# The first memory-key projection of a decoder trunk: one panel of 512 columns behind eight zero products

## The chip, the cores and the metric

The kernel runs on one core of one Trainium2 chip. A core has a matrix engine (TensorE, PE in the profile; its weight loads are PEld), a vector engine (VectorE, DVE), a scalar engine (ScalarE, ACT), GpSimd (POOL) and SyncE (SP). Each engine works through its own instructions in order. SP issues almost all transfers; ACT issues a few. The metric is the time of one execution on the device, in microseconds (us); less is better.

## The reference, cut to what matters

The reference is a two-layer decoder trunk on 256 tokens of width 2048. The first layer uses gated linear attention, the second a forgetting attention, and both also attend into 256 memory tokens. The change touches only how the memory keys of the first layer are made:

```python
mem_n = rmsnorm(mem, norm_mem)
for i in range(DEPTH):
    mk, mv = memory_kv(mem_n, mem_w_kv[i])      # (256 x 2048) @ (2048 x 1024): 512 columns of keys, 512 of values
    h = rmsnorm(x, norm_mix[i])
    x = x + mixer(h, mk, mv, ...)
    x = x + conv_ffn(rmsnorm(x, norm_ffn[i]), ...)
return rmsnorm(x, norm_final)
```

## The kernel before, in words

All weights lie in one packed array `wp`, in the order in which they are used, cut into panels and each panel into units of at most 128 x 1024 numbers (512 KB). `_panels` (line 51) lists the panels, `_layout` (line 108) their units. The first panels are: two panels of 256 columns for the keys of layer 0 (`mk`, 0, 0 and 0, 1), one of 512 columns for its values (`mv`, 0), then the same for layer 1, then the projections of the first mixer.

Every product is done in split precision. `load_unit` (line 178) loads a unit into `raw` and ACT rounds it to `whi` (line 189); `split_unit` (line 192) has DVE form the rest `wlo = raw - whi` (line 198). The activations are split the same way by `split` (line 283): ACT writes the high half (line 290), DVE the low half (line 291), side by side in one tile of 2 x 256. In a `proj_fm` panel (line 201) the weights are the stationary operand. For each of 16 chunks of 128 input rows and each block of 128 columns, `product` (line 220) issues two matmuls: `whi` against both halves (512 columns, line 223, or 226 for the last one) and `wlo` against the high half (256 columns, line 224). In this text such two matmuls are a **pair**. In a `proj_tm` panel (line 236) the activations are stationary and each chunk takes three matmuls of 512 columns for each of two blocks of tokens (lines 260 to 262).

Buffers: `raw` has 4, `whi` and `wlo` 3 each; the accumulators `acc` (pool `pacc`) are four banks of PSUM in all. A `proj_fm` panel takes two of them and a `proj_tm` panel two, so one panel's results can be read out while the next one is computed into the other two.

The start of the kernel (lines 404 to 466): `take_mem` (line 407) loads the memory tokens `mt`, in two pieces of two chunks and then three of four, each ahead of the weights that go with it, and splits them into `A`, scaled by the norm's gain from `gains`. The read-out of the first two panels is `mk_out` (line 415): ACT copies one half of the bank to `mk` (line 419), DVE adds the other half (line 420). Only after both is the bank free. `first_out` (line 432) also issues the squares of the memory tokens for its norm: four ACT squares of 128 x 1024 (line 439) and three DVE sums (line 441). Then the tokens `x` come in as 16 transfers of 128 KB (`xf`, line 451), and are split into `B` (line 456, through 290 and 291).

The order of instructions on each engine is fixed when the kernel is built, by a scheduler that is told priorities (`tc.high_priority`) and a few orderings (`tc.issue_after`); line order alone doesn't give it. Semaphores then hold each instruction until its inputs are there and its output buffer is free. A held instruction holds everything behind it on its engine. SP uses eight completion lanes in turn, so at most eight transfers are under way; a load of `raw` is also held until DVE has finished with the buffer's last unit.

Of the kernel before, what the change touches and what calls it, by code (L numbers as in the profile page):

```python
# [12 lines left out]
F32 = mybir.dt.float32  # L13
F32R = mybir.dt.float32r
I32 = mybir.dt.int32
AF = mybir.ActivationFunctionType
ALU = mybir.AluOpType
PSUM = bass.MemoryType.PSUM

P = 128  # L20
T = 256
D = 2048
KC = D // P
# [4 lines left out]
MEM_H = 4  # L28
# [9 lines left out]
AHEAD = 300  # L38

OG_EARLY = 2  # L40


G_Q, G_K, G_V = 0, 1024, 2048
# [7 lines left out]
def _panels():  # L51

    full = list(range(KC))
    out = []

    def fm(key, w, c0, kcs=full, second=None):
        cols = [(c0, 256)] if second is None else [(c0, 128), (second, 128)]  # L60
        out.append((key, w, kcs, cols, 4))

    def tm(key, w, c0, n, kcs=full):
        out.append((key, w, kcs, [(c0, n)], 2))

    for l in range(2):
        for j in range(2):
            fm(("mk", l, j), ("mem_w_kv", l), j * 256)
        tm(("mv", l), ("mem_w_kv", l), 512, 512)
    out.append((("glr",), ("gla_w_in", 0), full, [("twice", G_R, RANK)], 8))  # L70
    for j in range(2):
        fm(("mq", 0, j), ("gla_w_in", 0), G_MQ + j * 256)
    for h in range(GLA_H):
        fm(("gq", h), ("gla_w_in", 0), G_Q + h * DK)
        fm(("gk", h), ("gla_w_in", 0), G_K + h * DK)
        for j in range(OG_EARLY if h == GLA_H - 1 else 0):
            fm(("og", j), ("gla_w_in", 0), G_OG + j * 256)
# [24 lines left out]
    for f in range(4):  # L102
        tm(("wo", 1, f), ("fox_w_out", 0), f * 512, 512, late)
    ffn(1)
    return out
# [30 lines left out]
def _trunk(ctx: ExitStack, tc: tile.TileContext, xt, xtok, memt, wp, wgu, gns, gfin, cnv, par, msk, out):  # L136
    nc = tc.nc
# [6 lines left out]
    pacc = ctx.enter_context(tc.tile_pool(name="pacc", bufs=4, space=PSUM))  # L144
    pwork = ctx.enter_context(tc.tile_pool(name="pwork", bufs=1, space=PSUM))

    S.preload_act_table_set("natural_log_exp_and_others")
    gains = const.tile([P, G_N], F32, name="gains")
    with tc.high_priority(offset=2 * AHEAD):
        nc.sync.dma_start(gains, gns)  # L150
    part = const.tile([P, C_N], F32, name="part")
    mask = const.tile([P, M_N], F32, name="mask")
    ident = mask[:, M_ID : M_ID + P]
# [4 lines left out]
    def gain(name, i):  # L158
        c = C_GAIN[name] + i
        return gains[:, c : c + 1]  # L160
# [6 lines left out]
    bufB = [const.tile([P, 2, T], F32R, name=f"B{i}") for i in range(KC)]  # L167
    mk = [const.tile([P, MEM_H, T], F32, name=f"mk{l}") for l in range(2)]
    mv = [const.tile([P, 2, MEM_H * HD], F32, name=f"mv{l}") for l in range(2)]

    loads, casts = [], []

# [19 lines left out]
    def split_unit(unit, pieces=1, before=None, pool=wpool):  # L192
        with tc.high_priority(offset=AHEAD):
            raw, hi, w = load_unit(unit, pieces, before, pool)
            lo = pool.tile([P, NUNIT], F32R, name="wlo", tag="wlo", bufs=3)
            for i in range(pieces):
                s = slice(i * w // pieces, (i + 1) * w // pieces)
                V.tensor_tensor(lo[:, s], raw[:, s], hi[:, s].bitcast(F32), ALU.subtract)  # L198
        return hi, lo

    def proj_fm(key, src, evac, before=None):

        units = where[key]
        total = sum(len(u[1]) for u in units)
        acc = [pacc.tile([P, 512], F32, name="acc", tag="acc") for _ in range(2)]
        base = min(min(u[1]) for u in units)
        done = 0
        for n, unit in enumerate(units):
            if before is None:
                hi, lo = split_unit(unit)  # L210
            else:
                hi, lo = split_unit(unit, 1 if n else 2, lambda half: before(n, half))
            for j, kc in enumerate(unit[1]):
                for c in range(2):
                    product(acc[c], c, total - 1, done, src[kc - base], hi, lo, j)
                done += 1
        for c in range(2):
            evac(c, acc[c])

    def product(a, c, last, done, both, hi, lo, j):  # L220
        s = slice(j * 256 + c * P, j * 256 + (c + 1) * P)
        if done < last:
            TE.matmul(a, hi[:, s], both, start=done == 0, stop=False)  # L223
        TE.matmul(a[:, :T], lo[:, s], both[:, 0, :], start=False, stop=False)  # L224
        if done == last:
            TE.matmul(a, hi[:, s], both, start=False, stop=True)  # L226
# [177 lines left out]
    with tc.tile_pool(name="load", bufs=1) as lp:  # L404
        mt = [lp.tile([P, 4, T], F32, name=f"mt{i}") for i in range(4)]

        def take_mem(g, half):
            n = 2 if g == 0 else 4
            if n == 2 or half == 0:
                i = half * 2  # L410
                nc.sync.dma_start(mt[g][:, i : i + n, :], memt[g, :, i : i + n, :])
                for i in range(i, i + n):
                    split(bufA, 4 * g + i, mt[g][:, i, :], gain("mem", 4 * g + i))

        def mk_out(l, j):
            def evac(c, a):
                o = mk[l][:, 2 * j + c, :]
                if l == 0:
                    S.activation(o, a[:, T:], AF.Copy)
                    V.tensor_tensor(o, o, a[:, :T], ALU.add)  # L420
                    if c == 1 and j == 1:
                        for f in range(MEM_H):
                            V.tensor_tensor(mk[0][:, f, :], mk[0][:, f, :], nrm.row(), ALU.mult)
                else:
                    V.tensor_tensor(o, whole(a), nrm.row(), ALU.mult)

            return evac

        def mv_out(l):
            return lambda b, a: S.activation(mv[l][:, b, :], a, AF.Copy, scale=nrm.col()[:, b : b + 1])  # L430

        def first_out(c, a):
            mk_out(0, 0)(c, a)
            if c == 1:
                nc.sync.dma_start(mask[:, :M_FOX], msk[:, :M_FOX])
                sq, acc = [lp.tile([P, 4, T], F32, name=n) for n in ("sq4", "ssq4")]
                with tc.issue_after(casts[-1].ins):
                    for g in range(4):
                        S.activation(sq if g else acc, mt[g], AF.Square)
                        if g:  # L440
                            V.tensor_tensor(acc, acc, sq, ALU.add)
                V.tensor_tensor(acc[:, :2, :], acc[:, :2, :], acc[:, 2:, :], ALU.add)
                V.tensor_tensor(acc[:, 0, :], acc[:, 0, :], acc[:, 1, :], ALU.add)
                nrm.acc = acc[:, 0, :]

        proj_fm(("mk", 0, 0), bufA, first_out, before=take_mem)
        proj_fm(("mk", 0, 1), bufA, mk_out(0, 1))
        xf = [lp.tile([P, T], F32, name=f"xf{i}") for i in range(KC)]
        with tc.issue_after(loads[-1].ins):
            for i in range(KC):  # L450
                nc.sync.dma_start(xf[i], xt[i])
            nc.sync.dma_start(part, par)
            nc.sync.dma_start(mask[:, M_FOX:], msk[:, M_FOX:])
        proj_tm(("mv", 0), bufA, mv_out(0))
        for i in range(KC):
            split(bufB, i, xf[i], gain("mix0", i))
        for j in range(2):
            proj_fm(("mk", 1, j), bufA, mk_out(1, j))
            if j == 0:
                with tc.issue_after(loads[-1].ins):  # L460
                    for f in range(4):
                        nc.sync.dma_start(x[f], xtok[f])
                for f in range(4):
                    for b in range(2):
                        nx.add(f, b)
        proj_tm(("mv", 1), bufA, mv_out(1))
# [445 lines left out]
```

## Time and profile before

| | |
|---|---|
| three timed runs | 2315.9, 2314.12, 2314.14 us; median 2314.14 us |
| the profiled execution | 2315.51 us, of which the span from first to last instruction is 2313.7 us |
| DVE busy | 1608.0 us (69%) |
| ACT busy | 1254.2 us (54%) |
| DMA, mean over the span | 187 GB/s |
| mean granted TensorE clock | 0.998 |

All times inside the profile count from the span's start. A row of the timeline gives the start, the duration, the engine, the line in the kernel, the operation, the tile written and the tiles read, and how many like it follow one another; a bracket at its end tells how long the engine was idle before it and what it waited for. Durations of neighbours on one engine overlap by some tens of nanoseconds up to half of a matmul, so the pace of a row of instructions is read from start to start. The granted clock (PEclk) is the share of its full clock that TensorE was allowed.

### The profile page before, as it was taken

What the parts mean: (1) busy time and instruction counts of PE and PEld (TensorE: products, weight loads), DVE (VectorE), ACT (ScalarE), POOL (GpSimd) and SP (SyncE); (2) the same over time, 40 slices, a digit from 0 to 9 for tenths busy, and PEclk for the clock granted to TensorE, in tenths of its full rate; (3) what the DMA queues carried; (4) which work ended last, traced back from release to release, by engine and by line L of the source; (5) the groups of instructions that cost most, each with busy time, mean ns of one, the idle gap of its engine ahead of it and who ended that gap; (6) DMA issues with size and microseconds to landing.
All of it is one profiled execution on the core that took longest, in us unless ns stands there. A gap on an engine that the chain in (4) does not pass through costs nothing.

```text
span 2313.7 us, 32663 instructions
## 1 busy us (share of the span) xinstructions
PE 2296.8 (99%) x12190; PEld 1979.8 (86%) x12190; DVE 1608.0 (69%) x2595; ACT 1254.2 (54%) x1945; POOL 2.4 (0%) x17
## 2 busy tenths in 40 slices
PE   8999999999999999999999999999999999999998
PEld 7899998888888888888888888888888888888886
DVE  7577777567774777657767557657776577756775
ACT  6555555455553555445566445555554355534554
POOL 0000000000000000000000000000000000000000
PEclk9999999999999999999999999999999999999999
DMA  8645445555555555555556554455555555555554
GB/s 303 215 149 166 146 154 173 187 183 190 191 187 195 190 186 189 191 192 190 191 183 199 189 188 151 160 200 188 186 191 191 192 190 189 186 196 190 187 191 155
DMA packets 124167, 432.19 MB, mean 187 GB/s; under 512 B 14044, under 2 KB 18536, under 8 KB 123880
## 3 DMA queue, kind: packets, MB, share of 16 engines
q1 hardware_dynamic: 123720, 429.58, 56.3%
q8 instruction: 95, 1.56, 0.3%
q14 instruction: 64, 0.52, 0.1%
q10 hardware_dynamic: 288, 0.52, 0.1%
HBM read 427.94 MB, written 2.11 MB: 186 GB/s over the span
## 4 chain that ended last, share of the span: by engine, by line
PE 99%; DMA 0%; DVE 0%; ACT 0%; SPq 0%; issue 0%; DVEq 0%
PE acc L223 36%; PE acc L224 20%; PE acc L261 12%; PE acc L260 12%; PE acc L262 12%; PE acc L226 2%; PE ps_s L576 1%; PE ps_s L776 0%; PE ps_t L379 0%; PE acc L279 0%; PE ps_s L386 0%; PE ps_o L397 0%; DMA mt<-memt 0%; PE ps_s L690 0%; PE ps_o L706 0%; PE ps_o L590 0%
## 5 line engine op out<-in xcount | busy, mean ns | idle before, releaser
L198 DVE TENSOR_TENSOR wlo<-raw,whi 128x1024 fp32r<-128x1024 f32 (+2 forms) x801 | 971.5, 1213 | 555.8 <-ACT whi L189 540.8
L189 ACT ACTIVATE whi<-raw 128x1024 fp32r<-128x1024 f32 (+2 forms) x805 | 845.8, 1051 | 789.0 <-PE acc L262 385.1
L223 PE MATMUL acc<-B,whi 128*128 128x512 f32 x1980 | 685.7, 396 | 0.0
L223 PE MATMUL acc<-A,whi 128*128 128x512 f32 x1680 | 582.4, 397 | 6.9 <-DVE A L291 5.9
L224 PE MATMUL acc<-B,wlo 128*128 128x256 f32 x2112 | 551.4, 281 | 0.3 <-DVE wlo L198 0.3
L224 PE MATMUL acc<-A,wlo 128*128 128x256 f32 x1792 | 465.5, 282 | 0.5 <-DVE wlo L198 0.5
L223 PEld LDWEIGHTS acc<-B,whi 128*128 128x128 f32 x1980 | 361.1, 188 | 68.4
L224 PEld LDWEIGHTS acc<-B,wlo 128*128 128x128 f32 x2112 | 397.9, 188 | 21.6 <-DVE wlo L198 0.8
L223 PEld LDWEIGHTS acc<-A,whi 128*128 128x128 f32 x1680 | 306.7, 189 | 64.1 <-ACT whi L189 7.5
L224 PEld LDWEIGHTS acc<-A,wlo 128*128 128x128 f32 x1792 | 339.1, 189 | 21.0 <-DVE wlo L198 1.4
L261 PE MATMUL acc<-wlo,B 128*128 128x512 f32 (+1 forms) x704 | 268.9, 382 | 0.0
L262 PE MATMUL acc<-whi,B 128*128 128x512 f32 (+1 forms) x704 | 267.6, 381 | 0.0
L260 PE MATMUL acc<-whi,B 128*128 128x512 f32 (+1 forms) x704 | 242.8, 380 | 0.0
L261 PE MATMUL acc<-wlo,A 128*128 128x512 f32 x544 | 212.6, 391 | 0.0
L262 PE MATMUL acc<-whi,A 128*128 128x512 f32 x544 | 212.0, 390 | 0.0
L260 PE MATMUL acc<-whi,A 128*128 128x512 f32 x544 | 192.8, 391 | 0.0
L231 ACT ACTIVATE part<-acc 128x256 f32<-128x256 f32 x242 | 90.6, 374 | 161.5 <-PE acc L226 161.5
L261 PEld LDWEIGHTS acc<-wlo,B 128*128 128x128 f32 x704 | 132.2, 188 | 23.1
L262 PEld LDWEIGHTS acc<-whi,B 128*128 128x128 f32 x704 | 132.2, 188 | 22.6
L260 PEld LDWEIGHTS acc<-whi,B 128*128 128x128 f32 x704 | 131.7, 188 | 22.2
L233 DVE TENSOR_TENSOR wholes<-acc,part 128x256 f32<-128x256 f32 x242 | 101.9, 421 | 64.9 <-ACT part L231 64.7
L262 PEld LDWEIGHTS acc<-whi,A 128*128 128x128 f32 x544 | 102.1, 188 | 21.2
(195 smaller groups left out, 1590.2 us busy)
## 6 DMA issues: line engine op xcount, KB each, us to landing
raw<-wp SPq DMA_DIRECT2D x771, 512.0 KB, 3.3
raw<-wp SPq DMA_DIRECT2D x32, 384.0 KB, 3.0
xf<-xt SPq DMA_DIRECT2D x16, 128.0 KB, 4.7
x<-xtok SPq DMA_DIRECT2D x4, 512.0 KB, 6.2
mt<-memt SPq DMA_DIRECT2D x3, 512.0 KB, 8.7
cb<-cdram SPq DMA_DIRECT2D x12, 128.0 KB, 3.4
gf<-gfin SPq DMA_DIRECT2D x1, 1024.0 KB, 5.5
out<-x SPq DMA_DIRECT2D x4, 256.0 KB, 2.9
```

Source lines behind the costliest of these rows:

```text
L189: casts.append(S.activation(hi[:, s], raw[:, s], AF.Copy))
L198: V.tensor_tensor(lo[:, s], raw[:, s], hi[:, s].bitcast(F32), ALU.subtract)
L223: TE.matmul(a, hi[:, s], both, start=done == 0, stop=False)
L224: TE.matmul(a[:, :T], lo[:, s], both[:, 0, :], start=False, stop=False)
L226: TE.matmul(a, hi[:, s], both, start=False, stop=True)
L231: S.activation(t, a[:, T:], AF.Copy)
L233: V.tensor_tensor(r, a[:, :T], t, ALU.add)
L260: TE.matmul(a, xk[:, 0, xs], hi[:, s], start=u == 0 and j == 0, stop=False)
L261: TE.matmul(a, xk[:, 0, xs], lo[:, s], start=False, stop=False)
L262: TE.matmul(a, xk[:, 1, xs], hi[:, s], start=False, stop=last)
L576: TE.matmul(ps[:, b * NVER : (b + 1) * NVER], kt[:, c, b * P : (b + 1) * P], dd[:, 2 * c + b, :], start=c == 0, stop=c == 1)
```

## The change

The two first panels become one of 512 columns, laid out as `proj_tm` panels are: eight units of two chunks x 512 columns. The new `proj_first` takes all four banks at once and goes through the four blocks of 128 columns for each chunk; in the last unit it goes block by block, so that the first bank is finished first. The first two units and their memory tokens come in pieces of one chunk, the other memory tokens in pieces of two chunks. `mk_out` for layer 0 is folded into `first_out`. The first piece of memory tokens and the gains are issued from ACT's queue, and the load of the activation table follows them there. At the very start DVE fills the tile `B15` with zeros and TensorE does eight matmuls of 128 x 512 on it (`WARM = 8`), into a bank that nothing reads; `B15` gets its own data much later. All other panels keep their form.

```diff
+WARM = 8
...
     for l in range(2):
-        for j in range(2):
+        if l == 0:
+            tm(("mk", 0), ("mem_w_kv", 0), 0, 512)
+        for j in range(2 * l):
             fm(("mk", l, j), ("mem_w_kv", l), j * 256)
...
-    S.preload_act_table_set("natural_log_exp_and_others")
     gains = const.tile([P, G_N], F32, name="gains")
-    with tc.high_priority(offset=2 * AHEAD):
-        nc.sync.dma_start(gains, gns)
...
+    with tc.high_priority(offset=2 * AHEAD):
+        V.memset(bufB[KC - 1].bitcast(F32), 0.0)
+        warm = pwork.tile([P, 512], F32, name="ps_o", tag="o", bufs=1)
+        for i in range(WARM):
+            TE.matmul(warm, bufB[KC - 1][:, 0, :P], bufB[KC - 1], start=i == 0, stop=i == WARM - 1)
...
+    def proj_first(key, src, evac, before):
+
+        units = where[key]
+        acc = [pacc.tile([P, 512], F32, name="acc", tag="acc") for _ in range(4)]
+        for u, unit in enumerate(units):
+            hi, lo = split_unit(unit, 2 if u < 2 else 1, lambda piece: before(u, piece))
+            steps = [(c, j) for j in range(2) for c in range(4)]
+            if u == len(units) - 1:
+                steps.sort()
+            for c, j in steps:
+                product(acc[c], c, KC - 1, unit[1][j], src[unit[1][j]], hi, lo, j, 512)
+        for c in range(4):
+            evac(c, acc[c])
...
-    def product(a, c, last, done, both, hi, lo, j):
-        s = slice(j * 256 + c * P, j * 256 + (c + 1) * P)
+    def product(a, c, last, done, both, hi, lo, j, n=256):
+        s = slice(j * n + c * P, j * n + (c + 1) * P)
...
+        def take_mem(u, piece):
+            n = 1 if u < 2 else 2
+            i = 2 * u + piece
+            g = i // 4
+            eng = nc.scalar if i == 0 else nc.sync
+            eng.dma_start(mt[g][:, i % 4 : i % 4 + n, :], memt[g, :, i % 4 : i % 4 + n, :])
+            if i == 0:
+                nc.scalar.dma_start(gains, gns)
+                S.preload_act_table_set("natural_log_exp_and_others")
+            for i in range(i, i + n):
+                split(bufA, i, mt[g][:, i % 4, :], gain("mem", i))
...
         def first_out(c, a):
-            mk_out(0, 0)(c, a)
-            if c == 1:
-                nc.sync.dma_start(mask[:, :M_FOX], msk[:, :M_FOX])
...
+            o = mk[0][:, c, :]
+            S.activation(o, a[:, T:], AF.Copy)
+            V.tensor_tensor(o, o, a[:, :T], ALU.add)
+            if c < 3:
+                return
+            nc.sync.dma_start(mask[:, :M_FOX], msk[:, :M_FOX])
...
-        proj_fm(("mk", 0, 0), bufA, first_out, before=take_mem)
-        proj_fm(("mk", 0, 1), bufA, mk_out(0, 1))
+        proj_first(("mk", 0), bufA, first_out, take_mem)
```

More of the change, by code (lines that the diff above doesn't have):

```diff
@@ L199, in split_unit, with proj_fm @@
         return hi, lo
-    def proj_fm(key, src, evac, before=None):
+    def proj_first(key, src, evac, before):
[10 more added lines that the diff above has]
+            evac(c, acc[c])
+    def proj_fm(key, src, evac):
         units = where[key]
@@ L207, in proj_fm @@
         done = 0
[L208 to L212, printed above, removed]
+        for unit in units:
+            hi, lo = split_unit(unit)
             for j, kc in enumerate(unit[1]):
@@ L405, in _trunk, with mk_out @@
         mt = [lp.tile([P, 4, T], F32, name=f"mt{i}") for i in range(4)]
[L407 to L427, printed above, removed]
+        def take_mem(u, piece):
[9 more added lines that the diff above has]
+                split(bufA, i, mt[g][:, i % 4, :], gain("mem", i))
+        def mk_out(j):
+            return lambda c, a: V.tensor_tensor(mk[1][:, 2 * j + c, :], whole(a), nrm.row(), ALU.mult)
         def mv_out(l):
@@ L432, in first_out @@
         def first_out(c, a):
-            mk_out(0, 0)(c, a)
-            if c == 1:
-                nc.sync.dma_start(mask[:, :M_FOX], msk[:, :M_FOX])
[L436 to L444, printed above, removed]
-        proj_fm(("mk", 0, 0), bufA, first_out, before=take_mem)
-        proj_fm(("mk", 0, 1), bufA, mk_out(0, 1))
+            o = mk[0][:, c, :]
[4 more added lines that the diff above has]
+            nc.sync.dma_start(mask[:, :M_FOX], msk[:, :M_FOX])
+            sq, acc = [lp.tile([P, 4, T], F32, name=n) for n in ("sq4", "ssq4")]
+            with tc.issue_after(casts[-1].ins):
+                for g in range(4):
+                    S.activation(sq if g else acc, mt[g], AF.Square)
+                    if g:
+                        V.tensor_tensor(acc, acc, sq, ALU.add)
+            V.tensor_tensor(acc[:, :2, :], acc[:, :2, :], acc[:, 2:, :], ALU.add)
+            V.tensor_tensor(acc[:, 0, :], acc[:, 0, :], acc[:, 1, :], ALU.add)
+            nrm.acc = acc[:, 0, :]
+            for f in range(MEM_H):
+                V.tensor_tensor(mk[0][:, f, :], mk[0][:, f, :], nrm.row(), ALU.mult)
+        proj_first(("mk", 0), bufA, first_out, take_mem)
         xf = [lp.tile([P, T], F32, name=f"xf{i}") for i in range(KC)]
@@ L457, in _trunk @@
         for j in range(2):
-            proj_fm(("mk", 1, j), bufA, mk_out(1, j))
+            proj_fm(("mk", 1, j), bufA, mk_out(j))
             if j == 0:
```

## The prediction, as it was put on record

> **What bounds the kernel now.** The page comes first: TensorE is busy for nearly the whole span, and the chain that ended last is TensorE's own.
>
> ```profile
> span 2313.7 us, 32663 instructions
> ...
> PE 2296.8 (99%) x12190; PEld 1979.8 (86%) x12190; DVE 1608.0 (69%) x2595; ACT 1254.2 (54%) x1945; POOL 2.4 (0%) x17
> ...
> PE 99%; DMA 0%; DVE 0%; ACT 0%; SPq 0%; issue 0%; DVEq 0%
> ```
>
> So the time is TensorE's work plus whatever keeps it from working. The view of who waited for whom, for TensorE over the whole span, says where that is: 5.9 us until the first data, and 2.0 us in three short stops.
>
> ```profile
> PE acc L223 <- DVE A L291: 5.9, 1, 5.9
> PE acc L223 <- ACT whi L189: 1.1, 1, 1.1
> PE acc L224 <- DVE wlo L198: 0.9, 2, 0.5
> ```
>
> The view has no other row, and the stops lie in the first panel. There is a second loss, in the clock. In the timeline of the start a pair (512 and 256 columns) goes from start to start in 0.64 us at first (7.33 to 7.97), and in 0.346 us later (23.90 to 24.24).
>
> ```profile
> 5.88 1.22 PE L223 MATMUL acc<-A,whi 128*128 128x512 f32 x2 [5.88 <-DVE A L291]
> ...
> 7.33 0.63 PE L223 MATMUL acc<-A,whi 128*128 128x512 f32 x1
> ...
> 7.97 0.63 PE L223 MATMUL acc<-A,whi 128*128 128x512 f32 x1
> ...
> 12.01 0.73 PE L223 MATMUL acc<-A,whi 128*128 128x512 f32 x2 [1.05 <-ACT whi L189]
> ...
> 13.27 0.56 PE L224 MATMUL acc<-A,wlo 128*128 128x256 f32 x2 [0.53 <-DVE wlo L198]
> ...
> 22.85 0.62 PE L223 MATMUL acc<-A,whi 128*128 128x512 f32 x2
> ...
> 23.90 0.39 PE L223 MATMUL acc<-A,whi 128*128 128x512 f32 x1
> ...
> 24.24 0.39 PE L223 MATMUL acc<-A,whi 128*128 128x512 f32 x1
> ```
>
> The windows of 1 us show the same for the stretch after 13.6 us. Columns are each engine's busy time, then the granted clock, the share of DMA and its rate: TensorE had stopped for 1.05 us ahead of 12.01 and 0.53 us ahead of 13.27 (the brackets above), and from about 13.6 to 16.9, 3.3 us, the clock is 0.50.
>
> ```profile
> 12.00:13.00 1.00, 0.73 (x2) 0.30 (x2) 1.00 (x1) 1.00 (x3) 0.00 (x0) 1.00 1.05 430
> 13.00:14.00 1.00, 0.73 (x3) 0.69 (x4) 1.00 (x4) 1.00 (x3) 0.00 (x0) 0.78 1.02 415
> 14.00:15.00 1.00, 1.00 (x5) 0.85 (x4) 1.00 (x4) 1.00 (x3) 0.00 (x0) 0.50 1.02 403
> ...
> 16.00:17.00 1.00, 1.00 (x5) 0.90 (x4) 1.00 (x3) 1.00 (x2) 0.00 (x0) 0.51 1.06 397
> 17.00:18.00 1.00, 1.00 (x8) 0.87 (x7) 1.00 (x3) 1.00 (x2) 0.00 (x0) 1.00 0.95 373
> ```
>
> (Until 10 us the pair is as slow, though the clock column doesn't show it; there I go by the pair.) The first panel's 32 pairs would take 32 x 0.346 = 11.1 us and end at 22.85: start, stops and clock cost 11.8 us. That is what the change is aimed at, and all that it can gain.
>
> **The mark to compare with.** After both key panels comes the value panel:
>
> ```profile
> 31.70 0.62 PE L260 MATMUL acc<-whi,A 128*128 128x512 f32 x2
> ...
> 34.48 0.39 PE L261 MATMUL acc<-wlo,A 128*128 128x512 f32 x1
> ```
>
> Its first two products had been drawn forward to 31.70; without their 0.46 us the keys' 64 pairs would be done at 34.0. The instruction order of the changed kernel, with names and line numbers taken off, is that of the old one on all five engines behind the first value panel, but for a few swaps of neighbours. So the change is worth what the start of that panel moves against 34.0, plus what the clock does after it.
>
> **The change, part by part.**
>
> *ACT's queue at the start.* Two transfers move from SP to ACT, ahead of the table load.
>
> ```profile
> 0.73 1.28 ACT L147 ACT_TABLE_LOAD   x1 [0.73 <-PEq L903]
> ...
> 0.73 0.39 SPq L150 DMA_DIRECT2D gains<-gns  x1
> ...
> 4.40 0.91 ACT L290 ACTIVATE A<-mt,gains 128x256 fp32r<-128x256 f32 x2 [2.39 <-DMA mt<-memt]
> ...
> 5.22 0.61 ACT L189 ACTIVATE whi<-raw 128x512 fp32r<-128x512 f32 x1
> 5.86 0.69 DVE L198 TENSOR_TENSOR wlo<-raw,whi 128x512 fp32r<-128x512 f32 x1
> ```
>
> An issue takes some 0.4 us, the table 1.28; ACT was idle for 2.39 us ahead of 4.40, so 0.8 us of issues are hidden, and would delay the first product by 0.8 us without that cover.
>
> *The zeros.* No row has a fill on DVE; POOL's of the same size is the nearest:
>
> ```profile
> L475 POOL MEMSET ks<- 128x512 f32 x2 | 1.0, 528 | 0.0
> ```
>
> Bounds are 0.53 and, from DVE's own subtraction of that size, 0.69 us; I take 0.6. From 0.73 that gives 1.3; eight products of 512 columns (two thirds of a pair: 0.43 us each at the slow pace, 0.23 at the fast one) last until 4.8, or 3.2. TensorE is idle until 5.88, and DVE's first work waits for ACT's at 4.40, so both are free. Their worth is at most the slow pairs from 5.88 to 10 us, 4.1 x (1 - 0.346/0.64) = 1.9 us, at least nothing.
>
> *The first product.* It needs the first weights' piece (256 KB, now first in SP's queue), half as many tokens (128 KB) and the gains. Before, 304 KB had landed by 4.40. Now ACT rounds the weights (0.61) and then the tokens (0.49), DVE does 0.69 and 0.48 behind each: with weights at 4.0 and tokens and gains at 4.6, the first product starts at 5.8, as before. The finer pieces add four issues to SP and a few short instructions to ACT and DVE; these fall in the first 21 us, where ACT waits for landings again and again.
>
> *TensorE's own path.* From there 64 pairs x 0.346 = 22.1 us. I allow 1.8 us for stops while units two and three land. The first bank is full at about 27.7 and the panel ends at 29.7: 4.3 us ahead of 34.0. If nothing held the next panel, this would be the gain.
>
> *The banks.* But the panel holds all four banks, and the value panel's first product needs the first one back. Before, that panel had two banks that were long free. The read-out of the first bank is an ACT copy and then a DVE sum, and in the order of the changed kernel both stand far back. On ACT, from the first split of the tokens `xf`, stand ahead of the copy: twelve splits, three roundings of weights (the last key unit and two value units) and three squares of 128 x 1024. On DVE, behind the second square: two sums of 128 x 1024, two subtractions of weights and nine splits. Their pace, start to start, in the timeline of each engine:
>
> ```profile
> 23.05 1.06 ACT L189 ACTIVATE whi<-raw 128x1024 fp32r<-128x1024 f32 x1
> 24.02 0.36 ACT L419 ACTIVATE mk<-acc 128x256 f32<-128x256 f32 x1
> 24.28 1.70 ACT L290 ACTIVATE B<-xf,gains 128x256 fp32r<-128x256 f32 x4
> 25.88 1.05 ACT L439 ACTIVATE sq<-mt 128x1024 f32<-128x1024 f32 x1
> 26.83 1.05 ACT L189 ACTIVATE whi<-raw 128x1024 fp32r<-128x1024 f32 x1
> ```
>
> ```profile
> 24.14 1.22 DVE L198 TENSOR_TENSOR wlo<-raw,whi 128x1024 fp32r<-128x1024 f32 x1
> 25.29 0.41 DVE L420 TENSOR_TENSOR mk<-mk,acc 128x256 f32<-128x256 f32 x1
> 25.62 1.67 DVE L291 SCALAR_TENSOR_TENSOR B<-xf,gains,B 128x256 fp32r<-128x256 f32 x4
> 27.20 1.22 DVE L441 TENSOR_TENSOR ssq<-ssq,sq 128x1024 f32<-128x1024 f32 x1
> 28.34 1.22 DVE L198 TENSOR_TENSOR wlo<-raw,whi 128x1024 fp32r<-128x1024 f32 x1
> ```
>
> On ACT a rounding or a square is 0.96 and a split 0.40 us; on DVE a sum is 1.14, a subtraction 1.15, a split 0.395 (1.58 for four), a read-out sum 0.41.
>
> ACT can begin with those splits when `xf` is there. Ahead of its first piece go 0.05 MB of gains, 2.10 of memory tokens, 4.19 of weights and 0.13 of mask: 6.6 MB with itself. The rate in slots of 1 us, from 0 to 40:
>
> ```profile
> GB/s 0 30 167 309 254 186 225 377 360 397 426 410 430 415 403 412 397 373 324 127 266 334 310 344 204 274 397 345 359 243 312 332 279 216 228 326 367 393 369 340
> ```
>
> By 17 us 5.2 MB had moved; the slots from 12 to 17 have 0.41 MB per us. After that SP's loads were held for buffers (127 in the slot from 19); in the new order buffers come free earlier than their turn in the queue. Some of what has moved belongs to later transfers: 1.62 MB had been issued up to the tokens that let ACT go on at 9.30, when 2.0 MB had moved.
>
> ```profile
> 9.30 1.71 ACT L290 ACTIVATE A<-mt,gains 128x256 fp32r<-128x256 f32 x4 [0.77 <-DMA mt<-memt]
> ```
>
> So the first `xf` lands at 17 + (6.6 + 0.45 - 5.2)/0.41 = 21.5; I take 21.6. Then:
>
> - ACT reaches the copy at 21.6 + 12 x 0.40 + 6 x 0.96 = 32.2, 4.5 us after the bank was full.
> - Its second square ends at 21.6 + 1.2 + 3 x 0.96 + 0.1 = 25.8. DVE goes on from there: 2 x 1.14 + 2 x 1.15 + 9 x 0.395 = 8.1, at 33.9; the read-out sum ends at 34.3, and TensorE starts the value panel at 34.4.
>
> TensorE stands still from 29.7 to 34.4, 4.7 us, and **the whole lead of 4.3 us is gone**: 34.4 against 34.0 is +0.4 us. Bounds: if `xf` never held ACT, it would begin at 21.0 (after the rounding of the seventh unit), and if the two queues brought the first data 0.6 us earlier, all would: together -0.8 us. If `xf` lands as late as it did before, +2.8 us:
>
> ```profile
> xf<-xt SPq DMA_DIRECT2D x1, 128.0 KB, 4.9
> ```
>
> (issued at 19.06, landed 23.96, 2.4 us behind my figure).
>
> *The clock after the stop.* Stops of 1.05 and 0.53 us were followed by 3.3 us at 0.50. After 4.7 us I expect no less, and part of the next such stretch: some 4.3 us from the restart, each of which loses 0.46 us: 2.0 us. Bounds: nothing, and two stretches, 6.6 x 0.46 = 3.0. The value panel is TensorE's own work, and its weights land ahead of their use (same bytes, no later), so nothing hides this. The norm's own two products stand 34 products into that panel, at 34.4 + 34 x 0.23 = 42.2; DVE has their input 34.3 + 4 x 0.395 + 3 x 0.41 + 1.15 + 1.14 and two folds smaller than a sum later, by 40.6, and they wait for nothing.
>
> The Trainium skill (TensorE: Matmul & The Clock Gate, Part 1: The HAM clock gate) has the clock halved only after a whole idle window of about 3.4 us, on a grid that runs freely. The trace disagrees: 1.6 us in two stops sufficed. By the page a stop of 4.7 us may or may not hold a whole window, and the sum would be +0.4 or +2.4 us.
>
> **Sum.** +0.4 + 2.0 = +2.4 us. The profiled execution took 2315.51 us (span 2313.7 and 1.8 around it), 1.4 above the median of 2314.14; 1.4 is close to the 1.5 us that the slow stretch at 13.6 costs, which may be missing in two of the three runs. The new kernel would lose that part of its lead either way, since it waits for DVE. By the median it comes to 2316.5, by the profiled execution to 2317.9; I take **2317.0 us**, no change that a measurement of this kernel can tell (about 0.2%, 4.6 us).
>
> **The rivals.**
>
> - *The stop, but at full clock.* The throttle acts only on a stop that fills one whole stretch of 3.3 us; 4.7 us holds one in (4.7 - 3.3)/3.3 = 4 of 10 cases. For it: nothing in this trace; against it: the drop at 13.6. +0.4 us: 2314.5 to 2315.9, say 2315.
> - *No stop.* The banks come back in time because ACT and DVE run well ahead. It decides where DVE's read-out ends by 29.7, which needs 4.6 us less work ahead of it than the rows give. -4.3 us: 2309.8.
> - *Slower.* The transfer of `xf` sets the end: the splits of `xf` stand ahead of the read-out, and each microsecond that `xf` lands after 21.6 is one more. It counts as slower from a landing at about 23.9. For it: before, it landed at 23.96, in rows of 1 KB. Against: there it stood behind held loads. +2.8 + 2.0: 2318.9 by the median, 2320.3 by the profile.
> - *The zeros warm nothing.* The first pairs stay slow and the first bank is full at about 29.6 instead of 27.7; ACT still comes at 32.2. The time is the forecast's, 2317.
>
> **How the numbers follow.** Forecast 0.52, full clock 0.17, no stop 0.06, slower 0.17, cold zeros 0.08. The range leaves out "no stop" and the tails: from 2313.3 (full clock, bound of -0.8) to 2319.8 (late `xf`). Faster by over 0.2% (under 2309.5) is a part of "no stop": 0.04. Slower (over 2318.8) is most of the late `xf` and a little of the forecast: 0.14. Within: 0.82.
>
> **What would show it.** In the new profile: first product of data near 5.8; TensorE idle for 4 to 5 us ahead of the first product of the value panel (the activations-stationary line), ended by DVE's sum into `mk`; ACT's first copy into `mk` at 32 to 33; a clock of 0.50 in the microseconds after the stop; the second layer's key panel starting 2 us later than 56.75. I am wrong if that stop is under 2 us, if the clock stays at 1.00 behind it, or if TensorE stops anywhere after that panel.

## The result, and the profile after

Over 21 runs each, the new kernel takes 2318.48 us (2317.3 to 2319.81), the kernel before 2314.74 us (2313.43 to 2316.26). The ratio is 1.0016, with a 95% interval of 1.0011 to 1.0022: 3.74 us or 0.16% longer, under the 0.2% that was named as what counts. The forecast was 2317.0, in a range of 2313.3 to 2319.8. One single execution, of the kernel before with later splits (below), ran at a granted clock of 0.737 and took 2908.82 us; its ratio leaves it out.

The page of the new kernel, first:

```profile
span 2317.3 us, 32692 instructions
...
PE 2301.1 (99%) x12198; PEld 1982.4 (86%) x12198; DVE 1609.9 (69%) x2597; ACT 1254.6 (54%) x1946; POOL 2.4 (0%) x17
```

TensorE's busy time rose by 4.3 us for eight more matmuls. 3.8 of that are the zeros, ahead of the first data, where TensorE had been idle before, so busy time doesn't tell where the loss is. The waits of TensorE do:

```profile
PE acc L278 <- DVE mk L446: 4.5, 1, 4.5
...
PE acc L241 <- DVE A L309: 0.5, 1, 0.5
PE acc L242 <- DVE wlo L205: 0.5, 2, 0.3
```

The same view of before had 2.0 us in three stops, and the prediction put all three into the first panel. One of them lies far behind it, and the new kernel has it too (before, then new):

```profile
1265.22 0.38 PE L224 MATMUL acc<-B,wlo 128*128 128x256 f32 x1 [0.35 <-DVE wlo L198]
```

```profile
1268.64 0.39 PE L242 MATMUL acc<-B,wlo 128*128 128x256 f32 x1 [0.22 <-DVE wlo L205]
```

So the stops in the first panel were 1.6 us, and 0.3 are left in this execution. In their place stands one stop of 4.5 us, ahead of the value panel's first product (line 278, line 260 before), ended by DVE's sum into `mk`. In the timeline of TensorE (columns as before: start, duration, what, how many, and in brackets the idle time ahead):

```profile
1.45 3.78 PE L176 MATMUL ps_o<-B 128*128 128x512 f32 x8 [1.45 <-DVE B L173]
5.76 0.80 PE L241 MATMUL acc<-A,whi 128*128 128x512 f32 x1 [0.53 <-DVE A L309]
...
8.49 1.51 PE L241 MATMUL acc<-A,whi 128*128 128x512 f32 x4
...
28.45 0.40 PE L244 MATMUL acc<-A,whi 128*128 128x512 f32 x1
...
30.32 0.39 PE L244 MATMUL acc<-A,whi 128*128 128x512 f32 x1
35.26 0.80 PE L278 MATMUL acc<-whi,A 128*128 128x512 f32 x1 [4.55 <-DVE mk L446]
35.85 0.63 PE L279 MATMUL acc<-wlo,A 128*128 128x512 f32 x1
36.28 0.63 PE L280 MATMUL acc<-whi,A 128*128 128x512 f32 x1
...
41.05 0.39 PE L280 MATMUL acc<-whi,A 128*128 128x512 f32 x1
41.28 0.39 PE L278 MATMUL acc<-whi,A 128*128 128x512 f32 x1
...
56.48 0.59 PE L365 MATMUL ps_t<-dg,mask 128*128 128x256 f32 x2
...
60.35 0.62 PE L241 MATMUL acc<-A,whi 128*128 128x512 f32 x2
```

Line 244 is the last product of a bank, so the first bank is full at about 28.7 and the panel done at 30.7. The value panel starts at 35.26 (34.0 before, by the mark of the prediction), goes at 0.43 us a product at first (35.85 to 36.28) and later at 0.23 (41.05 to 41.28). The second layer's key panel starts at 60.35, 3.6 us after the 56.75 of before:

```profile
56.75 0.62 PE L223 MATMUL acc<-A,whi 128*128 128x512 f32 x2
```

That mark tells nearly the whole result. In the kernel before, the new one and every version below but one, the span ends 2256.9 to 2257.8 us after it; the exception comes with its experiment. Two things move by some tenths within these 0.9 us: the stop near 1265 us, and two products of the memory tokens' norm (on its tile `dg`, line 365, at 56.48 above), which stand ahead of the mark in some versions and behind it in others. They take 0.4 us: from 56.25 to 57.14 there are two other products, which would take 0.46 without them.

ACT and DVE over the same stretch, the rows that lead to the stop:

```profile
22.49 1.31 ACT L308 ACTIVATE B<-xf,gains 128x256 fp32r<-128x256 f32 x3 [0.53 <-DMA xf<-xt]
...
33.00 0.36 ACT L445 ACTIVATE mk<-acc 128x256 f32<-128x256 f32 x1
```

```profile
32.86 1.22 DVE L205 TENSOR_TENSOR wlo<-raw,whi 128x1024 fp32r<-128x1024 f32 x1
34.00 0.87 DVE L309 SCALAR_TENSOR_TENSOR B<-xf,gains,B 128x256 fp32r<-128x256 f32 x2
34.79 0.41 DVE L446 TENSOR_TENSOR mk<-mk,acc 128x256 f32<-128x256 f32 x1
```

The bank is full at 28.7; ACT comes to it at 33.00, DVE is through with it at 35.2. What stands before them are the splits of `xf`, which begin when `xf` lands, at 22.49, and the roundings, squares and sums among them; their numbers are those that the prediction counted. And the clock, in windows of 1 us (columns as before; the granted clock is the third number from the right):

```profile
33.00:34.00 1.00, 0.00 (x0) 0.00 (x0) 1.00 (x1) 1.00 (x4) 0.00 (x0) 0.65 0.99 403
34.00:35.00 1.00, 0.00 (x0) 0.00 (x0) 1.00 (x4) 1.00 (x5) 0.00 (x0) 0.50 1.00 410
...
40.00:41.00 1.00, 1.00 (x5) 0.77 (x5) 0.93 (x3) 0.00 (x0) 0.00 (x0) 0.94 0.86 324
```

Reading 0.65 as 0.30 us at full and the rest at half clock, the drop begins at 33.3, in the middle of the stop. It ends at 40.1, of which 4.9 us lie behind the restart.

### The profile page after: what moved, and what is told of

The parts are those of the page before. It is cut to its first block, busy times and chain, and to the rows that moved or that the text cites. A ratio compares the mean times of both kernels' runs of the same rounds, so it can differ in the third digit from the quotient of the medians.

```text
span 2317.3 us, 32692 instructions
## 1 busy us (share of the span) xinstructions
PE 2301.1 (99%) x12198; PEld 1982.4 (86%) x12198; DVE 1609.9 (69%) x2597; ACT 1254.6 (54%) x1946; POOL 2.4 (0%) x17
## 4 chain that ended last, share of the span: by engine, by line
PE 98%; DMA 1%; DVE 0%; ACT 0%; issue 0%; SPq 0%; DVEq 0%; ACTq 0%
PE acc L241 36%; PE acc L242 19%; PE acc L279 12%; PE acc L278 12%; PE acc L280 12%; PE acc L244 2%; PE ps_s L591 1%; DMA raw<-wp 1%; PE ps_s L791 0%; PE ps_t L397 0%; PE acc L297 0%; PE ps_s L404 0%; PE ps_o L415 0%; PE ps_s L705 0%; PE ps_o L721 0%; PE ps_o L605 0%
```

## The experiments

My theory after this profile: the loss is the stop (the banks come back late, because the splits of `xf` stand ahead of the read-out on both engines) and the half clock behind it. The rivals: that the new panel itself is slower, that the zeros cost something, that the stop costs nothing by itself. Each experiment was timed against the kernel before in the same batch; the kernel before came to 2313.88, 2314.33 and 2314.6 us in the three batches, so versions of different batches are compared through their ratio.

**Banks of its own for the value panel.** The two accumulators of that panel come from a pool that nothing else uses at this time; all work is done.

```diff
-    def proj_tm(key, src, evac, spare=None):
+    def proj_tm(key, src, evac, spare=None, own=None):
...
-        acc = [pacc.tile([P, 512], F32, name="acc", tag="acc") for _ in range(2)]
+        acc = own or [pacc.tile([P, 512], F32, name="acc", tag="acc") for _ in range(2)]
...
-        proj_tm(("mv", 0), bufA, mv_out(0))
+        proj_tm(("mv", 0), bufA, mv_out(0), own=[work("s", 2) for _ in range(2)])
```

> The value panel computes into two other banks of PSUM, so its first product waits for no read-out; ACT's and DVE's order is kept. Theory (the four banks are held by a read-out that stands far back on ACT and DVE): the stop of 4.5 us ahead of the value panel goes, and that panel starts at 30.6 instead of 35.3. DVE's queue is as long as before, so its subtractions for the third and fourth value unit come late and give back some 3 us in shorter stops: 2.5 to 4.5 us less than the changed kernel, 2314 to 2316. Rival (the wide panel costs by its transfers and pieces, not by its banks): no gain, 2318.5.

Measured: 2313.66 us, ratio 0.9998 (0.9989 to 1.0007). In TensorE's waits and timeline the stop is gone; the panel starts at 29.55, and waits 1.2 us for weights instead:

```profile
PE ps_s L279 <- DVE wlo L205: 1.2, 2, 1.0
```

```profile
29.55 0.62 PE L278 MATMUL ps_s<-whi,A 128*128 128x512 f32 x2
...
53.97 0.62 PE L241 MATMUL acc<-A,whi 128*128 128x512 f32 x2
```

With the banks there, +3.74 us against the kernel before becomes -0.2. So the wait for the banks carries the whole loss, the half clock included: the clock stays at 1.00 in this trace. But little of the new panel's lead shows in its place: TensorE now waits for weights, because ACT and DVE are still at the splits of `xf`. The value panel takes 53.97 - 29.55 = 24.42 us here; with those splits later as well, below, the wait is gone and it takes 22.23.

**The same work in another order: the splits of `xf` later.**

```diff
-            split(bufB, i, xf[i], gain("mix0", i))
+            with tc.issue_after(casts[min(i // 2, 5) - 6].ins):
+                split(bufB, i, xf[i], gain("mix0", i))
```

Here `casts` lists the roundings of weights issued so far; each pair of splits is put behind a later one, the last three pairs behind the same one.

> The changed kernel with the splits of xf ordered behind the value panel's third to eighth weights, two at a time. Theory: the read-out comes as soon as the banks are full, no stop at the value panel, no drop of the clock there: that panel starts at 30.6 against 34.0 before the change, 3.4 us less than the kernel before, 2311.3. Rival (the work is only moved, and TensorE stops for it in the value panel or in the key panel behind it): 2314 to 2318.

Measured: 2312.34 us, ratio 0.9994 (0.9985 to 1.0003). DVE's read-out comes at 30.45 instead of 34.79, and the stop shrinks from 4.55 to 0.48 us. Rows of DVE, then of TensorE:

```profile
30.45 0.75 DVE L446 TENSOR_TENSOR mk<-mk,acc 128x256 f32<-128x256 f32 x2
```

```profile
30.92 0.50 PE L278 MATMUL acc<-whi,A 128*128 128x512 f32 x1 [0.48 <-DVE mk L446]
...
53.32 0.62 PE L241 MATMUL acc<-A,whi 128*128 128x512 f32 x2
```

The clock stays at 1.00 around it. The banks are the same four as in the new kernel; only what stands ahead of the read-out is changed. So the stop is a matter of order on ACT and DVE. The time is 1.0 us above the 2311.3 that I expected. I had reckoned from the first trace of before, whose mark is 3.4 us later than this one; the mark of its second trace, below, is only 2.25 us later. In both, 0.4 us are the products of `dg`, which stand behind the mark here.

**Without the zeros.** `WARM`, the fill and the eight products are taken out (the block with `high_priority` in the diff above).

> The changed kernel without the fill of zeros and the eight products. Theory (DVE's queue sets the start of the value panel, whatever TensorE did before): the key panel ends later by up to 1.9 us, the stop is shorter by as much, the time stays at 2318.5, within 0.5. Rival (the zeros bring what they cost, on the path): 1 to 2 us more, 2320.

Measured: 2318.31 us, ratio 1.0019 (1.0010 to 1.0028): no difference to the new kernel. The stop is shorter, since the panel ends a little later and `xf` happened to land earlier (ACT's first split is at 21.24):

```profile
21.24 1.31 ACT L301 ACTIVATE B<-xf,gains 128x256 fp32r<-128x256 f32 x3 [0.53 <-DMA xf<-xt]
```

```profile
34.01 0.50 PE L271 MATMUL acc<-whi,A 128*128 128x512 f32 x1 [3.21 <-DVE mk L439]
...
58.45 0.61 PE L234 MATMUL acc<-A,whi 128*128 128x512 f32 x2
```

From the first split of `xf` to the value panel it is 34.01 - 21.24 = 12.77 us here, and 35.26 - 22.49 = 12.77 us in the new kernel. What TensorE does before the stop doesn't enter: `xf` sets the start of the value panel.

**The new kernel once more,** as a second trace of it.

> The changed kernel once more, to have it beside the next two: 3.7 us more than the kernel before, stop of 4 to 5 us at the value panel, low clock behind it.

Measured: 2318.59 us, ratio 1.0018 (1.0009 to 1.0026). In this execution the zeros did warm the clock (the first data product takes 0.50 us instead of 0.80), and the panel ended 0.8 us sooner:

```profile
5.75 0.50 PE L241 MATMUL acc<-A,whi 128*128 128x512 f32 x1 [0.52 <-DVE A L309]
...
34.52 0.79 PE L278 MATMUL acc<-whi,A 128*128 128x512 f32 x1 [4.59 <-DVE mk L446]
...
59.65 0.61 PE L241 MATMUL acc<-A,whi 128*128 128x512 f32 x2
```

The stop is as long as in the first trace, because `xf` happened to land 0.7 us sooner too: ACT's first split of it is at 21.75 here, and 34.52 - 21.75 is 12.77 us for the third time. The mark also comes 0.7 us sooner, yet the span is the same, 2317.3 us: the stop for weights near 1268 us takes 0.99 us in this execution, where it took 0.22.

**Products that fill the stop.** 18 and, in the next batch, 24 products of a tile of `A` into the unused bank stand behind the key panel. They compute nothing that is used.

```diff
+FILL = 18
...
+        for i in range(FILL):
+            TE.matmul(warm, bufA[KC - 1][:, 0, :P], bufA[KC - 1], start=i == 0, stop=i == FILL - 1)
```

> The changed kernel with 18 more products of 128x512 on A, into the bank that nothing reads, between the key panel and the value panel: TensorE works through the stop. Theory (the stop costs a second time through the clock): the clock stays at 1.00, the value panel still starts at about 35.3, and the time is 2.3 us less than the changed kernel's, 2316.2. Rival (the low clock after the stop isn't caused by the stop): 2318.5, or later if the products delay the panel.

> The changed kernel with 24 products in the stop, so that it is filled wholly also where the key panel ends early. Theory (low clock comes from the stop): no microsecond under 0.90 at the value panel, 1.5 to 2.5 us less than the changed kernel in the same call, unless the products outlast the stop (24 x 0.23 = 5.5 us, up to 1 us given back). Rival: no gain over the changed kernel.

Measured: with 18, 2317.56 us, ratio 1.0015 (1.0006 to 1.0024); with 24, 2317.93 us, ratio 1.0016 (1.0007 to 1.0025), 0.66 under the new kernel of the same batch. In the trace with 18, the clock doesn't drop and the value panel runs at its full pace:

```profile
29.77 4.26 PE L465 MATMUL ps_o<-A 128*128 128x512 f32 x18
34.59 0.50 PE L279 MATMUL acc<-whi,A 128*128 128x512 f32 x1 [0.55 <-DVE mk L447]
...
56.94 0.62 PE L242 MATMUL acc<-A,whi 128*128 128x512 f32 x2
```

ACT's first split of `xf` is at 21.82 in this trace, again 12.77 us ahead of the value panel. From its first product to the next panel the value panel takes 56.94 - 34.59 = 22.35 us here, and 60.35 - 35.26 = 25.09 in the new kernel. But 0.4 us of the difference are the two products of `dg`, which stand ahead of the mark in the new kernel and behind it here. With 24 they stand ahead of it too, the clock stays at 1.00 as well, and the panel takes 57.42 - 34.70 = 22.72 us:

```profile
34.70 0.40 PE L279 MATMUL acc<-whi,A 128*128 128x512 f32 x1
...
57.42 0.62 PE L242 MATMUL acc<-A,whi 128*128 128x512 f32 x2
```

So the half clock costs some 2.3 us in the traces (4.9 us, of which each loses 0.46 us, would be 2.3). The medians have won less than the 1.5 to 2.5 us that I expected: 0.66 us with 24, against the new kernel of its batch, and 0.75 with 18, against the version without zeros of its batch. Part of that can be seen in the profiled run with 18: its span ends 2258.4 us after the mark, about 1 us more than elsewhere (the stop near 1265 us takes 1.34 us), and 2.49 us lie around the span instead of 1.8. Over its eleven runs the time around the span goes from 1.76 to 3.13 us; by the median span, 18 products win 1.2 us (2315.3, where it is 2316.5 without zeros). The runs with 24 spread over 2316.59 to 2321.35 us, and the profiled one is the fastest of them. Why most of them win less than the trace is not settled. So it is shown that the drop comes from the stop; that it costs 2.3 us is shown by the traces, not by the medians.

**The kernel before, once more.**

> The kernel before, unchanged, profiled once more. Its times lie in two groups, near 2314.1 and near 2315.6, and the profile shown so far is of 2315.5. Theory: the groups differ by the drop of the clock at 13.6 us, so that a profile of the lower group has no 0.50 there and starts the second value-side key panel 1.5 us earlier. Rival: the groups differ by something behind the start; a profile of the lower group has the same start.

Measured: 2314.7 us in one run. TensorE's timeline shows nearly the same two stops as the first trace of before (0.91 and 0.52 us, where they were 1.05 and 0.53), and the windows show no drop, in this slot or a later one:

```profile
11.97 0.74 PE L223 MATMUL acc<-A,whi 128*128 128x512 f32 x2 [0.91 <-ACT whi L189]
13.24 0.50 PE L224 MATMUL acc<-A,wlo 128*128 128x256 f32 x2 [0.52 <-DVE wlo L198]
...
55.57 0.62 PE L223 MATMUL acc<-A,whi 128*128 128x512 f32 x2
```

```profile
13.00:14.00 1.00, 0.76 (x5) 0.72 (x6) 1.00 (x4) 1.00 (x3) 0.00 (x0) 1.00 1.00 409
```

So the low clock from 13.6 to 16.9 that the prediction was built on is an accident of that execution; without it the mark comes 56.75 - 55.57 = 1.2 us sooner. The time of this run lies between the two groups that I had seen, so it is not shown that the drop is what parts them.

**The kernel before, with the zeros alone.** `WARM` and the block with the fill and the products are put into the kernel before.

> The kernel before with the fill of zeros and the eight products alone. Theory (the zeros' part is the clock up to 10 us, and the old form has no stop that hides it): faster than before by 0.5 to 1.9 us. Rival (products of zeros don't count for the clock, or the pause behind them undoes them): no change, within 0.3 us.

Measured: 2314.97 us, ratio 1.0004 (0.9995 to 1.0013). The first data met a warm clock (0.74 us for two products instead of 1.22), and then TensorE waited longer for weights:

```profile
5.49 0.74 PE L230 MATMUL acc<-A,whi 128*128 128x512 f32 x2 [0.26 <-DVE A L298]
...
11.83 0.94 PE L230 MATMUL acc<-A,whi 128*128 128x512 f32 x2 [2.53 <-ACT whi L196]
```

The start of that product (12.01 and 11.97 without zeros) hardly moves. In the old form the landing of the second weights paces the first panel, and the zeros are worth nothing. They even make the stop longer, and here the clock dropped behind it (0.58, 0.50, 0.50 and 0.71 in the four slots from 12 us); the mark, 56.15, lies between the 55.57 and 56.75 without zeros. My expectation failed. The rival had the number, though not for its first reason: products of zeros did warm the clock.

**Both cures together, and three controls.** The last batch has four kernels: own banks and later splits at once; that with ten zero products instead of eight (`WARM = 10`); the later splits without any zeros; and the kernel before with the later splits.

> The new kernel with both edits at once: the value panel gets two banks of its own, and the splits of the tokens x go behind the weights. My theory says that the stop ahead of the value panel is one thing with one cause (the banks), so the two cures do not add: no stop at that place, the value panel starts at about 30.5, no low clock after it, the second layer's key panel starts at 53 to 54, and the time is within 0.8 us of the version that only moves the splits (2312.3), 2 us under the kernel before and 6 under the new one. The rival, that each edit cures something else (banks the stop, the order of the splits a wait for weights), has them add: another 1 us or more under the better of the two, 2311 or less.

> The same as the version with both edits, with ten products of zeros instead of eight, so that they last until the first data are there. My theory: in those executions in which the first data met a slow clock they now meet a full one, but the first panel is paced by what lands, so the time stays within 0.5 us of the version with eight. The rival, that TensorE's pace in the first 4 us sets when the panel ends: 1 to 1.9 us less than with eight.

> The version with the splits of x later, without the fill and the eight products of zeros. With the stop gone nothing swallows what the zeros win, if they win anything. My theory, that the landings pace the first panel: 0 to 0.7 us more than with zeros (2312.3 to 2313.0). The rival, that the slow pairs of the first 4 us are lost in full without zeros and saved in full with them: 1.5 to 1.9 us more (2313.8 to 2314.2).

> A control: the kernel before, with nothing changed but the order of the splits of x (behind the weights, as in the version of the new kernel that was faster). The kernel before has no stop at the value panel, so by my theory this order wins nothing there: within 0.5 us of before, and the gain of 2 us belongs to the panel of 512 columns once its stop is gone. The rival, that this order alone brings the gain whatever the panels' form: 1.5 to 2 us under before.

Measured, with the kernel before at 2314.6 us:

| version | us | ratio (interval) | second layer's keys start at |
|---|---|---|---|
| own banks, later splits | 2312.3 | 0.9990 (0.9981 to 0.9999) | 52.90 |
| the same, ten zeros | 2311.15 | 0.9985 (0.9976 to 0.9994) | 52.08 |
| later splits, no zeros | 2312.73 | 0.9992 (0.9983 to 1.0001) | 53.14 |
| before, later splits | 2314.04 | 0.9999 (0.9990 to 1.0008) | 55.24 |

In the last row the products of `dg` stand ahead of the mark, in the other three behind it.

The two cures hardly add (2312.3 against 2312.34 with the later splits alone; by the ratios to before, 0.9 us apart), which speaks for one cause. But 0.9 is close to the 1 us that the rival asked for, and the traces part them better: own banks bring the mark from 53.32 with the later splits to 52.90, and these 0.4 us are about what the later splits had left of the stop, 0.48 us. The order alone leaves the kernel before where it was, within what can be told (0.56 us less, just beyond the 0.5 that I expected): it gains where there is a stop to take away. Without zeros the later splits take 2312.73 instead of 2312.34, and by the ratios no more, so eight zeros are worth next to nothing here too. But ten zeros instead of eight win 1.15 us, and there my expectation (0.5 at most) failed and the rival held. The timeline with eight zeros, then with ten:

```profile
6.01 0.80 PE L241 MATMUL acc<-A,whi 128*128 128x512 f32 x1 [0.78 <-DVE A L309]
...
8.74 1.91 PE L241 MATMUL acc<-A,whi 128*128 128x512 f32 x4
...
30.67 0.62 PE L278 MATMUL ps_s<-whi,A 128*128 128x512 f32 x2
```

```profile
1.45 4.63 PE L176 MATMUL ps_o<-B 128*128 128x512 f32 x10 [1.45 <-DVE B L173]
5.91 0.80 PE L241 MATMUL acc<-A,whi 128*128 128x512 f32 x1
...
8.14 1.08 PE L241 MATMUL acc<-A,whi 128*128 128x512 f32 x4
...
29.84 0.62 PE L278 MATMUL ps_s<-whi,A 128*128 128x512 f32 x2
```

Four products of 512 columns take 1.91 us at 8.74 with eight zeros, and 1.08 at 8.14 with ten, where the first data product follows the zeros with no idle time in brackets. The first data product is still slow, 0.80 us; what is won comes behind it. As I read it, the finer pieces of the new panel land early enough that its pace at the start counts, unlike in the old form, and nothing behind it swallows the gain any more; the old form with ten was not run. This version is the best of all, 3.45 us under the kernel before, which is 0.15% and also under the 0.2% that was named as what counts.

## Why the prediction was right, point by point

- **ACT's queue and the first product:** right. 5.76, for 5.8.
- **The zeros:** right that they are worth nothing in this kernel (2318.31 without them), and so was the rival that they warm nothing, in the execution that was profiled. The reason is the one the prediction gave for that rival: ACT comes to the bank late either way. It didn't say that the zeros act in one execution and not in the next.
- **TensorE's own path:** the panel's end was put at 29.7; it came at 30.7, and at 29.9 in the second trace. The 1.8 us allowed for stops were too little and wrong in kind: beyond 64 pairs of 0.346 us the panel took 2.8 us more (30.7 - 5.8 - 22.1), of which 0.3 us were a stop and most of the rest the pairs up to about 9.4, which were still slow. In the second trace, where these pairs were fast, it took 2.1 more.
- **The banks:** right in mechanism, and nearly in size. Stop 4.7 us predicted, 4.55 measured; ACT at the bank at 32.2 predicted, 33.00 measured; from `xf` to the value panel 12.8 predicted (21.6 to 34.4), 12.77 measured four times. What was off is the landing of `xf`: 22.49 in the profiled execution for 21.6, and 21.82, 21.75 and 21.24 in others. That is 0.9 us of the error, and the start of the value panel came to +1.3 us instead of +0.4. That the length of the stop fits so closely is in part luck: both its ends came about 1 us late, for different reasons.
- **The clock:** right that it drops behind the stop. The size was 2.0 us; the value panel shows 2.3 against the kernel before (25.09, where 34.0 to 56.75 is 22.75), and 2.4 against the version with 24 products in the stop. The prediction allowed one stretch and a part of the next, 4.3 us from the restart; there were two in a row, which began inside the stop and reached 4.9 us past the restart.
- **The argument for the clock failed in part.** "1.6 us in two stops sufficed" holds for one execution: the second trace of before has nearly the same stops, 1.4 us, and no drop. The Trainium skill (TensorE: Matmul & The Clock Gate, Part 1: The HAM clock gate) says that the gate looks at windows of about 3.4 us on a grid of its own. The traces agree with that grid (low stretches of 3.42 and 6.8 us, as the last section shows); they don't agree that the window must be wholly idle.
- **The sum:** +1.3 + 2.3 = 3.6 us, which is 60.35 - 56.75 on the mark behind the panel, and 3.74 in the medians; predicted +2.4. That this pair of traces meets the medians so closely is luck: with the second traces of both kernels (59.65 and 55.57) the pairs give 2.9 to 4.8 us. The two terms that were too small are the landing of `xf` and the length of the half clock, and the time of 2318.48 us lies inside the range.
- **The signs.** The stop, what ended it, ACT's first copy at 33.00 and the low clock came as named, and the mark 3.6 us later instead of 2. "I am wrong if TensorE stops anywhere after that panel" came true by the letter, with the 0.22 us at 1268.64; but the kernel before had the same stop, and the prediction had taken it for one of the first panel.
- **The rivals.** "At full clock" did not come; its 4 in 10 rested on a stretch that must be filled whole, and here the stop began inside the window before the drop and the drop came all the same. "Slower by `xf`" had the right lever, only less of it: 0.9 us late, not 2.4. "No stop" was priced at -4.3 us, and the versions without a stop, or with less than 0.5 us of it, tell what it is worth: -0.2 us with own banks alone, -1.5 to -2.3 with the later splits (with or without zeros and own banks), -3.45 with ten zeros too. The price left out that the splits of `xf`, once the banks don't hold TensorE, hold the weights, and that the start is often still slow.

## What to carry to other kernels

A panel that takes all the accumulators at once moves the read-out onto the path: before doing it, list what stands ahead of the read-out on each engine that takes part, and put the work that the next panel doesn't need behind it. Price a stop of TensorE with the half clock that follows, here 2.3 us in the traces after a stop of 4.55, of which filling the stop won back 0.7 in the medians. A gain ahead of a wait with a fixed end is worth nothing until that wait is gone, so take the wait away first and measure the small gains again.

## What the runs showed of the hardware

The clock keeps to a grid of about 3.41 us in these traces. Worked out from the slots in which the clock changes (0.65 as 0.30 us full, and so on), the low stretches last 3.42 us in the first trace of before (13.56 to 16.98), 3.42 without zeros (34.84 to 38.26, rows below), and 6.8 in the new kernel (33.30 to 40.1), two of them.

```profile
34.00:35.00 1.00, 0.99 (x4) 0.85 (x5) 1.00 (x4) 1.00 (x3) 0.00 (x0) 0.92 0.95 307
...
38.00:39.00 1.00, 1.00 (x5) 0.78 (x5) 0.96 (x2) 0.00 (x0) 0.00 (x0) 0.87 0.85 303
```

The end of the slow start lies on the same grid: in the new kernel the pace changes at about 9.35 (the four products from 8.49 take 1.51 us, half way between 1.91 and 1.08), and 33.30 - 9.35 is 7 x 3.42; in the first trace of before it changes at about 10.1, one step ahead of 13.56. The clock records in the traces, of which the slots are means, say the same with more digits: in the new kernel full clock from 9.40 and half from 33.29 to 40.12, in the first trace of before 10.15, 13.56 and 16.97, without zeros 10.96, 34.85 and 38.26. Every difference is a whole number of steps of 3.413 us.

With that grid the other readings fall into place. The window ahead of the drop in the new kernel (29.9 to 33.3) still holds 0.8 us of work, and the one in before (10.15 to 13.56) holds 1.8 of 3.4, so it need not be idle throughout. In the second trace of before the window with both stops (10.92 to 14.33) holds 2.0 us of work, and no drop follows.

The zeros of 3.78 us are little longer than a window. Eight warm the clock where the grid happens to lie over them: it is full from 5.32 in the second trace of the new kernel, from 5.34 in the kernel before with zeros, from 4.30 with 24 products. Elsewhere the window that begins among them also holds the pause ahead of the data. With a pause of 0.53, 0.78 or 0.87 us (the new kernel, both cures, later splits) it left the clock slow; with one of 0.40 or 0.44 us (own banks, 18 products) it warmed it all the same. Ten run into the data without a pause, so that the first whole window, wherever it lies, is a busy one; in the one trace of them the clock is full from 7.53. This fits all the traces here, but how busy a window must be was not tried by itself.
